# State-space stage of a hybrid layer: pieces of the first projection in every second step, nine in a row, and the next preparation in their place in the others

## The chip, the cores and the metric

The kernel runs on one core of a Trainium2 chip, as one launch. The metric is the device time of that launch in microseconds (us), the median over runs. The engines of the core work side by side, each through its own queue in order: TensorE (PE, with PEld for the loading of weights), VectorE (DVE), ScalarE (ACT), GpSimd (POOL), and SyncE (SP), which issues most DMA transfers. They wait for each other by semaphores.

## What is computed

One layer of a decoder trunk on x of 1024 tokens by 1024 channels: two branches, a gated MLP with a chunked spatial gate (y_a) and a Mamba-2 state-space mixer (y_b), are projected, gated and merged. The stage at hand is the state-space mixer, and it shares its time with the first projection, y_a @ w_proj_a. The core of the reference:

```python
def ssd_scan(x, dt, a, bmat, cmat):
    ...
    a_cs = jnp.cumsum(adt, axis=-1)
    decay = segsum_exp(adt)
    cb = jnp.einsum('bclgn,bcsgn->bcgls', cc, bc)
    y_diag = jnp.einsum('bcgls,bcgrls,bcsgrp->bclgrp', cb, decay, xd)
    decay_to_end = jnp.exp(a_cs[..., -1:] - a_cs)
    chunk_states = jnp.einsum('bcsgn,bcgrs,bcsgrp->bcgrpn', bc, decay_to_end, xd).astype(jnp.float32)
    chunk_decay = jnp.exp(a_cs[..., -1])
    def step(state, inp):
        cs, cd = inp
        return state * cd[..., None, None] + cs, state
    ...
    y_off = jnp.einsum('bclgn,bcgrpn,bcgrl->bclgrp', cc, prev_states, jnp.exp(a_cs))
    return (y_diag + y_off).reshape(b, s, h, p).astype(x.dtype)
...
    y_b = y_b + xh * d_skip[:, None]
    yz = (y_b.reshape(b, s, SSM_D_INNER) * jax.nn.silu(ssm_z)).reshape(b, s, SSM_GROUPS, SSM_D_INNER // SSM_GROUPS)
    y_b = rms_norm(yz, ssm_norm_w.reshape(SSM_GROUPS, -1)).reshape(b, s, SSM_D_INNER)
    merged = jax.nn.sigmoid(g_a) * (y_a @ w_proj_a) + jax.nn.sigmoid(g_b) * (y_b @ w_proj_b)
```

There are 8 groups of 4 heads of width 64, a state of 128, and 8 chunks of 128 tokens.

## The kernel before

**Steps.** The state-space stage goes in 32 steps, n = 0 to 31. A step is one group and two chunks (256 tokens, s = 0 to 3). Groups go in pairs: an even n is the first group of a pair, the odd n behind it the second, and s advances every second step. So n = 8r + 2s + j is group 2r + j at s; n = 10 is group 2, s = 1, and its tiles carry the ending 2_1 (yi2_1). At s = 3 (n = 6, 7, 14, 15 and so on) only one chunk state is added, since nothing follows it; at s = 0 only the second chunk has a state to read.

**Parts of a step.** `front` (L1173): PE multiplies the masked decay with the inputs (yi, 8 products, from dcy and xd) and makes the chunk states (sp, from xe and bn). The DVE adds sp to the running state (add_state, L1214 and L1216), and joins yi with the skip term into y1 (L1196); POOL multiplies the state by its chunk decay (mul_state, L1208). Where a group's squares are ready, `front` also makes the short product pq that sums them over the channels. `back` (L1220): PE makes yn from the states before each chunk, the DVE multiplies it by the decays (ym, L1242), POOL adds y1 (y, L1244) and gates the sum (yz, L1245). `prep` (L1150) readies a later step: PE makes pc (the product of C and B, and B turned) and px (x turned), the DVE multiplies the decay by pc (dcy, L1163) and px by two factors (xd, xe, L1166), and ACT copies the turned B (bn, L1170). `ahead_of` (L1543) writes, between the parts, the decay exponentials of step n+2 on ACT (L1147, eight per step; `decays(n + 3)` makes all below n+3), the state product of the next step on POOL, one of the waiting side jobs (squares on ACT, L1269; their sum on POOL, L1273; roots, L1300), and the mask of step n+3 (ACT, L1135; POOL, L1139). `fetch` (L1115) loads inputs of later steps.

**Order.** On DVE, ACT and POOL these operations are linked (`link`, L1091): each engine keeps them in the order in which they are written. PE's products stand in program order too. A scheduler places the rest. The products write to PSUM, which has 8 buffers of 512 numbers per partition; `bank` (L510) hands one out per product, six in one ring and two in another, and a product must wait until the last reader of its buffer's former tile is done.

**Pieces.** `proj_a` (L1481) is the first projection cut into pieces: each is two products of 128x128 by 128x512 into the tiles pma (192 pieces in all, 24 for each of 8 blocks). `draw` (L1534) puts some of them into the stream of PE. At the end of a block the DVE forms tha (L1506); early in a block it also makes the split weights of the next (wal, L1400, in `wa_lows`; the ACT part, L1395, in `wa_block`). The loop of before (L1557 to L1572) draws 4 pieces in an even step and 5 in an odd one, between front and back, and prepares step n+2 after back. After the loop the rest of the pieces is drawn, and the second projection (p1) begins with eight PSUM buffers taken in a written order (L1816).

Of the kernel before, what the change touches and what calls it, by code (L numbers as in the profile page):

```python
# [8 lines left out]
F32 = mybir.dt.float32  # L9
# [7 lines left out]
P = 128  # L17
# [18 lines left out]
def hybrid_kernel(  # L36
# [1444 lines left out]
    def proj_a():  # L1481

        for dd in range(KT):
            if dd + 2 < KT:
                wa_load(dd + 2)
            ths, pms = [], []
            for h in range(2):
                th = turn(tha_r, f"tha{dd}_{h}", F32)
                load(th, th_d[dd * P : (dd + 1) * P, h * 512 : (h + 1) * 512])
                ths.append(th)  # L1490
                pms.append(bank(f"pma{dd}_{h}"))
            for k in range(KT):
                wh, wl = was[dd][k // 4]
                yh, yl = yas[k]
                ks = slice(k % 4 * P, (k % 4 + 1) * P)
                for n, (lw, r) in enumerate(((wh, yh), (wh, yl), (wl, yh))):
                    for h in range(2):
                        mm(pms[h], lw[:, ks], r[h], k + n == 0, k == KT - 1 and n == 2)
                    yield
                if k == 1 and dd + 1 < KT:  # L1500
                    wa_block(dd + 1)
                elif k == 3 and dd + 1 < KT:
                    wa_lows(dd + 1)
            keep = pin if dd == KT - 1 else lambda i: i
            for h in range(2):
                keep(V.scalar_tensor_tensor(ths[h], ths[h], 1.0, pms[h], op0=ALU.add, op1=ALU.mult))  # L1506
            for h in range(2):
                keep(nc.scalar.dma_start(mt_d[dd][:, h * 512 : (h + 1) * 512], ths[h]))
# [25 lines left out]
    def draw(n):  # L1534
        for _ in range(n):
            left[0] -= next(fill, 1) is None
# [21 lines left out]
    for n in range(2):  # L1558
        step(n, "front")
        ahead_of(n)  # L1560
        draw(10)
    for n in range(len(order)):
        if n > 1:
            step(n, "front")
            ahead_of(n)
            draw(6 if n == 2 else 4 + n % 2)
        step(n, "back")
        if n == 1:
            draw(4)
        if n + 2 < len(order):  # L1570
            step(n + 2, "prep")
        fetch(n + 6)  # L1572
    while tasks or work or posts:
        draw(2)
# [238 lines left out]
    for u, (nm, k) in enumerate(units):  # L1813
        if k == 0:
            if nm == "p1":
                first = {t: psb.tile([P, 512], F32, name=f"{t}p", tag=f"b{t}") for t in ('x0', 'x1', 'x2', 'x3', 'y3', 'y1', 'y2', 'y0')}  # L1816
                psx, psy = ([first[f"{v}{j}"] for j in range(4)] for v in "xy")
            elif nm in ("p5", "p2"):
                psy = banks(f"y{nm}", "y")
            ps = psy if nm in ("p2", "p5", "p3") else psx  # L1820
        multiply(u, ps)
        ahead(u)
        if nm == "p1" and k == 2:
            for tags, _ in (y1_r, ym_r):
                room.extend(tags)
        if nm == "p1" and k in (1, 4):
            for late in groups[NG - 2 :]:
                late.post4() if k == 4 else late.post3()
            if k == 1:
                for late in groups[NG - 2 :]:  # L1830
                    late.root()
        if nm == "p2" and k == 4:
            room.extend(rb_r[0])
        if k % 2 and nm in GATES:
            gate_load(GATES[nm][0] + k // 2, GATES[nm][1])
        if nm == "p4":
            for at, f, a in BESIDE:
                if at == k:
                    f(*a)
        if nm in ("p7", "p2", "p4") and k % 2 == (nm != "p4"):  # L1840
            merged(*more.pop(0))
        if k == KT - 1:
            for j in range(4):
                with tc.high_priority():
                    if nm in ("p1", "p3", "p5"):
                        t = slot_tile(f"{nm}_{j}")
                        A.copy(t, (psx if nm == "p1" else psy)[j])
                        sums[nm, j] = t
                    if nm == "p6":
                        V.tensor_add(sums["p3", j], sums["p3", j], psx[j])  # L1850
                    elif nm == "p5":
                        V.tensor_add(sums["p3", j], sums["p3", j], sums["p5", j])
                        more.append((j, 1, sums["p3", j], f"p3_{j}"))
                    elif nm == "p7":
                        V.tensor_add(sums["p5", j], sums["p5", j], psx[j])
                        more.append((4 + j, 1, sums["p5", j], f"p5_{j}"))
                    elif nm == "p2":
                        V.tensor_add(sums["p1", j], sums["p1", j], psy[j])
                        more.append((j, 0, sums["p1", j], f"p1_{j}"))
                    elif nm == "p4":  # L1860
                        merged(4 + j, 0, None, None)
# [179 lines left out]
```

## Time and profile before

| what | value |
|---|---|
| median of 3 runs | 1365.81 us (1364.84 to 1366.97) |
| profiled execution | 1369.39 us |
| its span on the core | 1367.4 us |
| its mean granted TensorE clock | 0.998 |
| state-space steps 2 to 29 (935.15 to 1107.16) | 172.01 us |
| mean step | 172.01 / 28 = 6.14 us |

The profile shows one execution. The span is what the trace covers of its own time. A timeline row gives start, length, engine, source line, operation, output and inputs with their shapes, and in square brackets how long the engine was idle before it and what ended that. The names of the tiles are given without their numbers, so yn stands for the yn of every step. An x behind a row is the number of instructions that follow each other without a gap. A source line L82 or L85 is that of a helper that issues all products, so products are told apart by their tiles. POOL is idle in most of the span and busy in the state-space stage, so its share of the whole span says little of that stage.

### The profile page before, as it was taken

Reading aid. Unit: us, or ns where it says so; the run is one execution under the profiler, and the core shown is the slowest. Engines: PE = TensorE matmul, PEld = TensorE weight load, DVE = VectorE, ACT = ScalarE, POOL = GpSimd, SP = SyncE. Lnnn points to the kernel's source line nnn. Section 1 sums busy time; section 2 is a strip of 40 time slices with the busy share of each in tenths; the row PEclk is TensorE's granted clock in tenths of the full one; section 3 lists DMA queues with packets and bytes.
Section 4 is the critical chain, followed back from the end, with each engine's and each line's share of the span. In section 5 each row is a group of like instructions: output and inputs, shape, how many; then the busy total and the mean of one; then the engine's idle time right before and its main releaser. Section 6 shows DMA issues by size and latency. Waiting matters only on the chain.

```text
span 1367.4 us, 20180 instructions
## 1 busy us (share of the span) xinstructions
PE 1352.4 (99%) x6943; PEld 1117.4 (82%) x6943; DVE 1047.6 (77%) x1720; ACT 799.6 (58%) x1449; POOL 195.4 (14%) x191
## 2 busy tenths in 40 slices
PE   8999999999999999999999999999999999999997
PEld 7688888888888888888888888888888888888886
DVE  4786886777778898688887788457888866959976
ACT  5763666666656665465576665486877834233443
POOL 1000000000000000000000000016798971000002
PEclk9999999999999999999999999999999999999999
DMA  9675444343344657877665865488889958988913
GB/s 287 180 232 142 147 124 123 100 126 113 116 131 139 204 179 227 257 228 239 203 197 180 260 196 182 155 308 273 300 299 313 306 200 311 333 266 322 379 41 123
DMA packets 249530, 288.65 MB, mean 211 GB/s; under 512 B 16812, under 2 KB 196436, under 8 KB 249428
## 3 DMA queue, kind: packets, MB, share of 16 engines
q1 hardware_dynamic: 174868, 203.80, 46.9%
q10 hardware_dynamic: 74560, 83.57, 17.9%
q8 instruction: 55, 0.90, 0.3%
q14 instruction: 47, 0.39, 0.1%
HBM read 199.82 MB, written 87.49 MB: 210 GB/s over the span
## 4 chain that ended last, share of the span: by engine, by line
PE 90%; DVE 3%; DMA 3%; issue 1%; SPq 1%; ACT 1%; POOL 0%; POOLq 0%; DVEq 0%; ACTq 0%
PE xx L565 6%; PE xcb L565 6%; PE xz L565 6%; PE xuz L565 6%; PE xg L565 5%; PE pma L82 5%; PE ox L1885 3%; PE yuz L565 3%; PE yx L565 3%; PE ycb L565 3%; PE vx L970 3%; PE yp L1694 3%; PE yz L565 3%; PE yg L565 3%; PE yi L82 2%; PE sp L82 2%
## 5 line engine op out<-in xcount | busy, mean ns | idle before, releaser
L1139 POOL TENSOR_SCALAR_AFFINE_SELECT dcy<-dcy 128x1024 f32<-128x1024 f32 x32 | 37.7, 1179 | 788.0 <-DMA yl<-ya_d 744.6
L1147 ACT ACTIVATE dcy<-dcy,nacs 128x128 f32<-128x128 f32 x256 | 78.2, 389 | 4.9 <-POOL dcy L1139 4.2
L1163 DVE TENSOR_TENSOR dcy<-dcy,pc 128x1024 f32<-128x1024 f32 x32 | 39.0, 1220 | 9.0 <-PE pc L85 8.0
L1245 POOL TENSOR_TENSOR yz<-y,sl 128x512 f32<-128x512 f32 x32 | 44.3, 1386 | 2.5
L82 PE MATMUL pma<-yh,wah 128*128 128x512 f32 x128 | 43.1, 418 | 0.0
L82 PE MATMUL pma<-yh,wal 128*128 128x512 f32 x128 | 42.5, 413 | 0.0
L1040 ACT ACTIVATE ac<-ac 128x1024 f32<-128x1024 f32 x32 | 34.0, 1061 | 13.5 <-DVE ac L1038 13.3
L1170 ACT COPY bn<-pc 128x256 f32<-128x256 f32 x32 | 11.9, 372 | 49.8 <-DVE dcy L1163 49.8
L1632 DVE SCALAR_TENSOR_TENSOR yn<-yn,par,rb 128x512 f32<-128x512 f32 x32 | 25.2, 786 | 20.1 <-DMA yn<-yb_d 18.8
L82 PE MATMUL pma<-yl,wah 128*128 128x512 f32 x128 | 40.2, 395 | 0.0
L1135 ACT ACTIVATE ea<-dcy 64x512 f32<-64x512 f32 x64 | 39.8, 622 | 0.4
L1244 POOL TENSOR_TENSOR y<-y,ym 128x512 f32<-128x512 f32 (+1 forms) x32 | 37.0, 1156 | 3.5 <-DVE ym L1242 3.1
L1038 DVE SCALAR_TENSOR_TENSOR ac<-c2x,cwt,ac 128x1023 f32<-128x1023 f32 (+2 forms) x24 | 30.7, 1280 | 7.3 <-ACT ac L1036 7.2
L1038 DVE SCALAR_TENSOR_TENSOR ac<-c2cb,cwt,ac 128x1023 f32<-128x1023 f32 (+2 forms) x24 | 30.7, 1280 | 6.8 <-ACT ac L1036 6.6
L1242 DVE TENSOR_TENSOR ym<-yn,ea 128x512 f32<-128x512 f32 (+1 forms) x32 | 19.9, 623 | 19.9 <-PE yn L82 19.7
L82 PE MATMUL yi<-dcy,xd 128*64 128x128 f32 x512 | 35.0, 279 | 0.0
L82 PEld LDWEIGHTS yn<-sl,st 128*128 128x128 f32 x224 | 30.4, 195 | 5.3 <-POOL st L1208 2.8
L1900 POOL TENSOR_TENSOR r<-r,fnw 128x512 f32<-128x512 f32 x4 | 5.3, 1342 | 204.4 <-ACT junk L1898 204.4
L82 PE MATMUL yn<-sl,st 128*128 128x128 f32 x224 | 30.9, 278 | 2.4 <-POOL st L1208 2.4
L840 ACT CAST wbb<-wbr 128x512 fp32r<-128x512 f32 x32 | 19.8, 618 | 22.5 <-DMA wb_d<-wbb 18.9
L82 PE MATMUL sp<-xe,bn 128*128 128x256 f32 x112 | 32.7, 409 | 0.0
L1002 ACT ACTIVATE vm<-vm,vr 128x128 f32<-128x128 f32 x64 | 25.7, 483 | 11.3 <-DMA vm<-v_d 10.9
(2975 smaller groups left out, 4380.2 us busy)
## 6 DMA issues: line engine op xcount, KB each, us to landing
sl<-s_d SPq DMA_DIRECT2D x32, 768.0 KB, 6.7
s_d<-ac ACTq DMA_DIRECT2D x32, 512.0 KB, 3.6
wb_d<-wbb ACTq DMA_DIRECT2D x32, 512.0 KB, 3.6
dcy<-acs_d SPq DMA_DIRECT2D x32, 512.0 KB, 5.6
av<-in_w_in_dram SPq DMA_DIRECT2D x36, 256.0 KB, 3.2
aw<-in_ada_w_dram SPq DMA_DIRECT2D x16, 512.0 KB, 6.5
wbr<-in_w_proj_b_dram SPq DMA_DIRECT2D x32, 256.0 KB, 4.6
yb_d<-yz ACTq DMA_DIRECT2D x32, 256.0 KB, 6.0
```

The costliest lines, as they stand in the source:

```text
L82: pin(PE.matmul(acc, l, r, start=first, stop=last))
L565: pin(PE.matmul(ps, lw[:, k * P : (k + 1) * P], r[k], start=first and n + k == 0, stop=n == 2 and k == 3, skip_group_check=not first))
L970: pin(PE.matmul(ps[pn][j], l[:, j * P : (j + 1) * P], r, start=nm in ("p1", "p5", "p2") and n + units[i][1] == 0, stop=n == 2 and k == 3, ...
L1038: V.scalar_tensor_tensor(ac[:, s:], cc[:, : S - s], conv_wt[:, 3 - s, i : i + 1], ac[:, s:], op0=ALU.mult, op1=ALU.add)
L1135: link("A", lambda: A.activation(ea[hh * HD : (hh + 1) * HD], dcy.rearrange("p (j e) i l -> p e j (i l)", e=2)[hh * HD : (hh + 1) * HD, hh ...
L1139: link("G", lambda: G.affine_select(out=d8, in_=d8, compare_op=ALU.is_ge, fill=-1e30, base=0, pattern=[[0, 2 * HPG], [1, P]], channel_mult ...
L1147: link("A", lambda: A.activation(dcy[:, h, i, :], dcy[:, h, i, :], AF.Exp, bias=sub[:, i, h : h + 1]))
L1163: link("V", lambda: V.tensor_tensor(d3, d3, pc[:, 0:256].unsqueeze(1).to_broadcast([P, HPG, 256]), op=ALU.mult))
L1244: link("G", lambda: G.tensor_add(y1[:, :, t0:], y1[:, :, t0:], m[:, :, t0:]))
L1245: link("G", lambda: G.tensor_mul(yz, y1, sl[:, 4:6]))
L1694: pin(PE.matmul(ps[j], a[:, v, js], r, start=first and n + k == 0, stop=n == 2 and k == KT - 1, skip_group_check=not first))
L1885: pin(PE.matmul(ps, a[:, tsl], b[:, cs], start=first and n + j == 0, stop=n == 2 and j == 3, skip_group_check=not first))
```

## The change

The main loop treats even and odd steps apart from n = 2 on. An even step draws no piece; there the preparation of step n+2 stands between `ahead_of` and `back`. An odd step draws nine pieces (eleven at n = 3) between front and back, and prepares step n+2 after back as before. Through the loop as many pieces are drawn as before, and no operation is added or removed on any engine. For the first block alone the split of the next block's low weights is written after the sixth instead of the fourth eighth of the block. And the eight buffers of the second projection are taken in another order.

```diff
-                elif k == 3 and dd + 1 < KT:
+                elif k == (3 if dd else 5) and dd + 1 < KT:
                     wa_lows(dd + 1)
...
+    def prepare(n):
+        if n < len(order):
+            step(n, "prep")
+
     for n in range(len(order)):
+        even = n > 1 and n % 2 == 0
         if n > 1:
             step(n, "front")
             ahead_of(n)
-            draw(6 if n == 2 else 4 + n % 2)
+        if even:
+            prepare(n + 2)
+        elif n > 1:
+            draw(11 if n == 3 else 9)
         step(n, "back")
         if n == 1:
             draw(4)
-        if n + 2 < len(order):
-            step(n + 2, "prep")
+        if not even:
+            prepare(n + 2)
         fetch(n + 6)
...
-                first = {t: psb.tile([P, 512], F32, name=f"{t}p", tag=f"b{t}") for t in ('x0', 'x1', 'x2', 'x3', 'y3', 'y1', 'y2', 'y0')}
+                first = {t: psb.tile([P, 512], F32, name=f"{t}p", tag=f"b{t}") for t in ('x0', 'x1', 'y3', 'x2', 'y0', 'y2', 'y1', 'x3')}
```

Three places show what this does to the engines. The first is PE in step 10. Before, the chunk states sp2_1 are followed by four pieces, then yn of the step, then the preparation of step 12 (pc2_2):

```order
L82 MATMUL sp2_1_9173<-xe2_1_9079,bn2_1_9081 128x256 x2
L82 MATMUL pma2_0_8812<-yh60_8166,wal2_1_8566 128x512
L82 MATMUL pma2_1_8815<-yh61_8167,wal2_1_8566 128x512
L82 MATMUL pma2_0_8812<-yh70_8172,wah2_1_8565 128x512
L82 MATMUL pma2_1_8815<-yh71_8173,wah2_1_8565 128x512
L82 MATMUL pma2_0_8812<-yl70_8174,wah2_1_8565 128x512
L82 MATMUL pma2_1_8815<-yl71_8175,wah2_1_8565 128x512
L82 MATMUL pma2_0_8812<-yh70_8172,wal2_1_8566 128x512
L82 MATMUL pma2_1_8815<-yh71_8173,wal2_1_8566 128x512
L82 MATMUL yn2_1_9205<-sl2_1_8851,st22_8278 128x128 x2
L82 MATMUL yn2_1_9205<-sl2_1_8851,st_8275 128x128 x2
L82 MATMUL pc2_2_9217<-sl2_2_9007 128x128
```

In the changed kernel, from the same product on:

```order
L82 MATMUL sp2_1_9173<-xe2_1_9061,bn2_1_9063 128x256 x2
L82 MATMUL pc2_2_9198<-sl2_2_9007 128x128
L85 MATMUL pc2_2_9198<-ident_135,sl2_2_9007 128x128
L85 MATMUL px2_2_9197<-ident_135,sl2_2_9007 128x128 x2
L82 MATMUL pc2_2_9198<-sl2_2_9007 128x128
L85 MATMUL pc2_2_9198<-ident_135,sl2_2_9007 128x128
L85 MATMUL px2_2_9197<-ident_135,sl2_2_9007 128x128 x2
L82 MATMUL yn2_1_9214<-sl2_1_8851,st22_8278 128x128 x2
L82 MATMUL yn2_1_9214<-sl2_1_8851,st_8275 128x128 x2
L82 MATMUL yi3_1_9230<-dcy3_1_8912,xd3_1_9151 64x128 x8
L82 MATMUL pq0_1_9239<-yz0_2_8744,ones_140 32x128 x4
L82 MATMUL sp3_1_9246<-xe3_1_9153,bn3_1_9155 128x256 x2
```

The four pieces are gone from between sp and yn, the preparation of step 12 stands there, and yi of step 11 follows yn directly; pq0_1 is the sum of squares that the front of step 11 makes.

The second place is the DVE in the same step, from the skip term y1 of step 10 on. Before:

```order
L1196 SCALAR_TENSOR_TENSOR y12_1_9178<-sl2_1_8851,dskt_151,yi2_1_9164 128x256 x2
L1506 SCALAR_TENSOR_TENSOR tha2_0_8810<-tha2_0_8810,pma2_0_8812 128x512
L1506 SCALAR_TENSOR_TENSOR tha2_1_8813<-tha2_1_8813,pma2_1_8815 128x512
L1216 TENSOR_TENSOR st21_8277<-st21_8277,sp2_1_9173 128x256
L1242 TENSOR_TENSOR ym2_1_9210<-yn2_1_9205,ea2_1_8853 128x512
L1163 TENSOR_TENSOR dcy2_2_9005<-dcy2_2_9005,pc2_2_9217 128x1024
L1166 TENSOR_TENSOR xd2_2_9227<-px2_2_9216,dthq_154 128x512
L1166 TENSOR_TENSOR xe2_2_9229<-px2_2_9216,dde_155 128x512
```

In the changed kernel:

```order
L1196 SCALAR_TENSOR_TENSOR y12_1_9178<-sl2_1_8851,dskt_151,yi2_1_9164 128x256 x2
L1216 TENSOR_TENSOR st21_8277<-st21_8277,sp2_1_9173 128x256
L1163 TENSOR_TENSOR dcy2_2_9005<-dcy2_2_9005,pc2_2_9198 128x1024
L1166 TENSOR_TENSOR xd2_2_9208<-px2_2_9197,dthq_154 128x512
L1166 TENSOR_TENSOR xe2_2_9210<-px2_2_9197,dde_155 128x512
L1242 TENSOR_TENSOR ym2_1_9219<-yn2_1_9214,ea2_1_8853 128x512
L1285 TENSOR_SCALAR cwt_148<-pq0_1_9239 128x128
L1216 TENSOR_TENSOR st_8275<-st_8275,sp3_1_9246 128x256
L1196 SCALAR_TENSOR_TENSOR y13_1_9251<-sl3_1_8914,dskt_151,yi3_1_9230 128x256 x2
```

The three operations on the preparation of step 12 (dcy2_2, xd2_2, xe2_2), which stood behind ym of step 10, now stand ahead of it, and so ahead of the state and y1 of step 11 as before; the two tha of the block have moved behind those.

The third place is POOL around the sum of squares of group 3 (yz3_0, L1273), in steps 15 and 16. Before:

```order
L1273 TENSOR_TENSOR yz2_0_9061<-yz2_0_9061 128x512
L1139 AFFINE_SELECT dcy5_0_9419<-dcy5_0_9419 128x1024
L1244 TENSOR_TENSOR y12_3_9515<-y12_3_9515,ym2_3_9547 128x512
L1245 TENSOR_TENSOR yz2_2_9394<-y12_3_9515,sl2_3_9161 128x2x256
L1300 TENSOR_TENSOR ssq_158<-ssq_158,nhalf_144 128x8
L1139 AFFINE_SELECT dcy4_1_9498<-dcy4_1_9498 128x1024
L1244 TENSOR_TENSOR y13_3_9594<-y13_3_9594,ym3_3_9626 128x512
L1245 TENSOR_TENSOR yz3_2_9474<-y13_3_9594,sl3_3_9235 128x2x256
L1208 TENSOR_TENSOR st21_8277<-st_8275,cd_157 128x256
L1273 TENSOR_TENSOR yz3_0_9135<-yz3_0_9135 128x512
```

In the changed kernel:

```order
L1300 TENSOR_TENSOR ssq_158<-ssq_158,nhalf_144 128x8
L1139 AFFINE_SELECT dcy5_0_9403<-dcy5_0_9403 128x1024
L1244 TENSOR_TENSOR y12_3_9515<-y12_3_9515,ym2_3_9556 128x512
L1245 TENSOR_TENSOR yz2_2_9397<-y12_3_9515,sl2_3_9161 128x2x256
L1273 TENSOR_TENSOR yz2_0_9068<-yz2_0_9068 128x512
L1139 AFFINE_SELECT dcy4_1_9498<-dcy4_1_9498 128x1024
L1244 TENSOR_TENSOR y13_3_9579<-y13_3_9579,ym3_3_9620 128x512
L1245 TENSOR_TENSOR yz3_2_9474<-y13_3_9579,sl3_3_9227 128x2x256
L1208 TENSOR_TENSOR st21_8277<-st_8275,cd_157 128x256
L1273 TENSOR_TENSOR yz3_0_9135<-yz3_0_9135 128x512
```

The sum of group 2's squares (yz2_0) and a root (ssq, L1300) have changed places: the sum now stands one step later, only five operations ahead of the sum of group 3.

## The prediction

> **What bounds the kernel now.** I read the page first: its span and its busy row for TensorE.
>
> ```profile
> span 1367.4 us, 20180 instructions
> PE 1352.4 (99%) x6943; PEld 1117.4 (82%) x6943; DVE 1047.6 (77%) x1720; ACT 799.6 (58%) x1449; POOL 195.4 (14%) x191
> ```
>
> TensorE sets the end, so the change can win only TensorE work or TensorE waits. The windows view, over the stretch that the change rearranges (start of step 2 to start of step 30; the columns are length, PE, PEld, DVE, ACT, POOL, clock, DMA share, GB/s), and the waits view for PE around it (905 to 1130) say what is there to win:
>
> ```profile
> 935.15:1107.16 172.01, 172.01 (x1381) 146.74 (x1380) 142.75 (x254) 128.81 (x342) 148.14 (x145) 1.00 0.87 294
> ...
> PE yn L82 <- POOL st L1208: 2.4, 1, 2.4
> PE pq L82 <- POOL lq L1265: 0.3, 1, 0.3
> ```
>
> PE is busy for all 172.01 us, 172.01 / 28 = 6.14 us a step, at the full granted clock. The two waits lie outside (at 928 and in the tail). VectorE and GpSimd, at 83% and 86% of the stretch, are close behind. So the state-space loop holds no wait that the change could remove, and two engines have less than 1.1 us of slack a step.
>
> **How a step is paced.** The timeline of step 10, which starts at T = 984.21 with its yi, up to the first products of step 11:
>
> ```profile
> 984.15 1.22 DVE L1163 TENSOR_TENSOR dcy<-dcy,pc 128x1024 f32<-128x1024 f32 x1 [0.51 <-PE pc L85]
> 984.21 1.09 PE L82 MATMUL yi<-dcy,xd 128*64 128x128 f32 x16
> 984.59 1.09 POOL L1139 TENSOR_SCALAR_AFFINE_SELECT dcy<-dcy 128x1024 f32<-128x1024 f32 x1 [2.36 <-ACT ea L1135]
> 985.23 1.13 PE L82 MATMUL sp<-xe,bn 128*128 128x256 f32 x4
> 985.29 0.68 DVE L1166 TENSOR_TENSOR xd<-px,dthq 128x512 f32<-128x512 f32 x1
> 985.41 0.37 ACT L1170 COPY bn<-pc 128x256 f32<-128x256 f32 x1 [0.89 <-DVE dcy L1163]
> 985.80 1.15 ACT L1269 ACTIVATE yz<-yz 128x512 f32<-128x512 f32 x2
> 985.89 0.68 DVE L1166 TENSOR_TENSOR xe<-px,dde 128x512 f32<-128x512 f32 x1
> 986.01 0.81 PE L82 MATMUL pma<-yh,wal 128*128 128x512 f32 x2
> 986.46 1.30 POOL L1245 TENSOR_TENSOR yz<-y,sl 128x512 f32<-128x512 f32 x1
> 986.65 0.63 PE L82 MATMUL pma<-yh,wah 128*128 128x512 f32 x2
> 986.86 2.14 ACT L1147 ACTIVATE dcy<-dcy,nacs 128x128 f32<-128x128 f32 x7
> 987.12 0.62 PE L82 MATMUL pma<-yl,wah 128*128 128x512 f32 x2
> 987.71 1.18 POOL L1208 TENSOR_TENSOR st<-st,cd 128x256 f32<-128x256 f32 x2
> 988.04 1.05 PE L82 MATMUL yn<-sl,st 128*128 128x128 f32 x8
> 988.86 1.28 POOL L1273 TENSOR_TENSOR yz<-yz 128x512 f32<-128x512 f32 x1
> 988.91 0.39 ACT L1147 ACTIVATE dcy<-dcy,nacs 128x128 f32<-128x128 f32 x1
> 988.93 0.39 PE L82 MATMUL pc<-sl 128*128 128x128 f32 x2
> 990.13 1.09 PE L82 MATMUL yi<-dcy,xd 128*64 128x128 f32 x16
> 991.15 0.43 PE L82 MATMUL pq<-yz,ones 128*32 128x128 f32 x8
> ```
>
> From starts to starts: yi and sp take 986.01 - 984.21 = 1.8 us, a pair of pieces' rows 0.47 (986.65 to 987.12), yn 0.89 (988.04 to 988.93), a preparation (pc, px) 1.20 (988.93 to 990.13), yi alone 1.02 (990.13 to 991.15). The pieces are the cover: while PE multiplies them, ScalarE makes the decays of step 12 (done at 988.91 + 0.39 = 989.30 = T+5.09), which the DVE needs for the preparation of step 12 (PE does it at T+4.72, DVE right behind). GpSimd works through its queue without a gap up to 990.14 = T+5.93.
>
> **The change, part by part.** The same products, copies and pieces run, so no engine's work changes. What changes is where TensorE has cover. An even step now goes yi, sp, preparation, yn with no piece: 1.8 + 1.2 + 0.9 = 3.9 us, say 4.0, until yi of the next step, and 5.0 until what follows that yi. The odd step gets nine pieces, 18 rows or some 4.2 us, and is 8.2 us long. The preparation of n+2 is asked of PE at T+1.9 instead of T+4.7, but its DVE and ACT part can't come earlier: the decay of n+2 is finished at T+5.09 where squares (L1269) stand before it, and without them as in step 4, where T is 948.37:
>
> ```profile
> 948.37 1.09 PE L82 MATMUL yi<-dcy,xd 128*64 128x128 f32 x16
> 949.96 1.28 ACT L1147 ACTIVATE dcy<-dcy,nacs 128x128 f32<-128x128 f32 x4
> ...
> 943.45 2.45 ACT L1147 ACTIVATE dcy<-dcy,nacs 128x128 f32<-128x128 f32 x8
> ```
>
> that is at 949.96 + 2.45 = 952.41 = T+4.04. Behind it come dcy (1.14 from start to start), xd (0.60), xe (0.68), and bn (0.37) on ACT. So the buffer of px is free only at T+6.5 (7.5 with squares) and that of pc at about T+5.7 (6.6). Meanwhile PE hands out PSUM buffers at twice the pace, and ym(n), which waits only for yn, is now queued behind that trio on the DVE. In the built order each product takes a certain buffer; these are the places where its last reader is late, and the stalls they give:
>
> Step 10: pq0_1 takes the buffer of px2_2, the preparation just made. Wanted at T+5.0; free at 5.09 + 1.14 + 0.60 + 0.68 = T+7.5. 2.4 us; and px2_2 itself takes that of px3_1, whose xe ends at 985.89 + 0.68 = T+2.36, wanted at T+2.2: 0.2.
>
> Step 28: sp7_2, in the front of step 29, takes the buffer of px6_3. Wanted at T+5.4, since a pq (0.43) stands in step 28's front; free at T+6.5: 1.1 us.
>
> Step 26: sp7_1, in the front of step 27 behind a pq, takes the buffer of pc6_2: wanted at T+5.4, bn at T+6.6. 1.2 us.
>
> Steps 16 and 24: the pq in the odd step's front is now wanted at T+5.0, and the sum (L1273) it reads is the last of GpSimd's queue; in step 10 that ended at T+5.93, at 16 and 24 it starts later because the y product before it waited for the late ym and another sum stands ahead: 0.9 at least, 1.28 + 0.9 = 2.2 at most, 1.4 taken for each: 2.8 us. Steps 18 and 26 have the same with one sum: 0.3 each, 0.6.
>
> Step 20: the pc of step 22 takes the buffer of step 21's px: its xe at T+2.4 to T+2.8 against T+2.2: 0.4.
>
> Steps 2, 6 and 30 need rows of their own, of the timeline in step 2 (T = 935.15) and step 30 (T = 1107.16):
>
> ```profile
> 935.15 1.09 PE L82 MATMUL yi<-dcy,xd 128*64 128x128 f32 x16
> 938.12 0.37 ACT L1170 COPY bn<-pc 128x256 f32<-128x256 f32 x1 [5.21 <-DVE dcy L1163]
> 939.20 0.41 DVE L1216 TENSOR_TENSOR st<-st,sp 128x256 f32<-128x256 f32 x1
> 939.53 0.86 DVE L1196 SCALAR_TENSOR_TENSOR y<-sl,dskt,yi 128x256 f32<-128x256 f32 x2
> ...
> 1107.16 1.09 PE L82 MATMUL yi<-dcy,xd 128*64 128x128 f32 x16
> 1108.54 0.81 PE L82 MATMUL pma<-yh,wal 128*128 128x512 f32 x2
> 1109.45 0.41 DVE L1216 TENSOR_TENSOR st<-st,sp 128x256 f32<-128x256 f32 x1
> 1109.78 0.86 DVE L1196 SCALAR_TENSOR_TENSOR y<-sl,dskt,yi 128x256 f32<-128x256 f32 x2
> ```
>
> Step 2, where the DVE comes late from earlier work: yn is wanted at T+3.0 and takes the buffer of pc (bn ends at 938.49 = T+3.34), its second half waits for the state (939.61 = T+4.46), and the next yi for y1 (940.39 = T+5.24). 0.3 + 0.7 + 0.3 = 1.3 us. Step 6, a short front like step 30's: PE is through yi and sp at T+1.4, through the preparation at T+2.6, and yn takes the buffer of its own yi, which y1 frees at 1110.64 = T+3.48: 0.9. Step 30 has no preparation left: yn follows at T+1.4, its second half at T+1.85 waits for the state at 1109.86 = T+2.70: 0.85.
>
> The sum is 2.4 + 0.2 + 1.1 + 1.2 + 2.8 + 0.6 + 0.4 + 1.3 + 0.9 + 0.85 = 11.75 us. A stalled pair of steps starts the next pair late on all engines alike, so a stall isn't paid back by the odd step: PE has no gap there to give up. The other side: 14 fewer runs of pieces. The first pair of a run shows 986.65 - 986.01 = 0.64 instead of 0.47 us, 0.17 more; but it begins while the rows of sp still run (985.23 + 1.13 = 986.36), so most of that is overlap. Between 0 and 14 x 0.17 = 2.4 us I take 0.6, near the low end. The later wal subtractions of the second block, the tail's first buffers and the fetches add no instruction and no transfer, and leave PE's products in place: nothing, and 1 us at most for a late first product of the tail. That makes 11.75 - 0.6 = +11.1 us. Against the profiled execution's span it is 1367.4 + 11.1 = 1378.5 (1380.5 with what lies around it, 1369.39); against the median of the runs, 1365.81, it is 1376.9.
>
> **A stall may cost more than itself.** After the one long wait of before, the rows ran at half rate:
>
> ```profile
> 928.37 1.17 PE L82 MATMUL yn<-sl,st 128*128 128x128 f32 x4 [2.38 <-POOL st L1208]
> 929.32 0.63 PE L82 MATMUL pc<-sl 128*128 128x128 f32 x2
> 929.75 0.42 PE L85 MATMUL pc<-ident,sl 128*128 128x128 f32 x1
> 932.02 0.70 PE L82 MATMUL pma<-yh,wal 128*128 128x512 f32 x2
> ```
>
> pc's pair took 929.75 - 929.32 = 0.43 us to the next product, where a whole preparation of 10 such rows takes 1.20. From 928.4 to 932.0 work went at half speed, some 1.6 us lost for 2.38 us idle. The Trainium skill, "TensorE: Matmul & The Clock Gate", section "HAM oscillation — how this bites in real kernels", gives an idle gap above about 3.4 us as what brings the slow clock. By that rule none of the stalls summed here would cost clock. By the row above, the one at step 10 (2.4 us) might, and the sum would be 1378.5; the rule is not borne out by that row.
>
> **The rivals.** First, stalls that drop the clock: three of them (steps 10, 16, 24) at 1.6 us: 1376.9 + 4.8 = 1381.7. For it speaks the row after 2.38 us; against it that only one stall is as long as that.
>
> Second, all is hidden, 1365.8: were the decays of n+2 made a step sooner, px and pc would be free in time. ACT has 172.01 - 128.81 = 43 us of idle time for that, but its order is written, the decay behind bn of the step before, and the sums on GpSimd would stay late; it decides if the trio on the DVE is done by T+5.0.
>
> Third, faster: the start of a run is a real loss on PE, halving the 28 runs brings the whole 2.4 us, the 0.3 us wait of pq in the tail goes too, and the buffers are free in time after all: 1365.8 - 2.7 = 1363.1. It decides where the stalls together stay under 2.7 us. For it speaks the 0.17 us in the row, against it the overlap.
>
> Fourth, a part of it: only the waits for buffers of px and pc and for the states stay and GpSimd's are hidden, since its queue may run ahead: 11.1 - 3.4 = 7.7: 1373.5. This is part of my forecast's own range.
>
> **How the numbers follow.** The forecast, slower without loss of clock, has 0.62 (the fourth case in it); with loss of clock 0.17; hidden 0.09; faster 0.12. A difference of 0.2%, 2.7 us, is about what a measurement of this kernel tells from none. The third case ends at that bound, so 0.08 of it counts as faster and 0.04 as the same: faster 0.08, same 0.13, slower 0.79. The likeliest one's own range is 1371 (the stalls half as long) to 1381 (each GpSimd wait at its bound of 2.2). It is widened to the clock case above, and below until the hidden and the faster case are left out, which with what lies above make two in ten: 1368.5 to 1384.
>
> **What would show it.** In the profile after, PE's waits in this stretch should be some 9 to 14 us instead of none: pq on the DVE's xe (L1166) with about 2.4 us, pq on GpSimd's L1273 twice over 1 us, yn on the DVE's L1216 and L1196, sp on bn and xe in the last steps; each pair of steps 12.3 us plus its stalls, and the stretch from step 2 to step 30 about 182 us. A granted clock under 1.00 there would show the clock case. If waits stay under 3 us, the forecast is wrong at its root, that the late decay holds the buffers; if they are there but the time isn't longer, the start of a run of pieces was mis-sized.

## The result, and the profile after

| | before | after |
|---|---|---|
| median of the runs (5 each, in turn on one chip) | 1365.81 us (1364.84 to 1366.97) | 1379.44 us (1378.70 to 1380.84) |
| profiled execution | 1369.39 us | 1379.44 us |
| its span | 1367.4 us | 1377.6 us |

The changed kernel takes 1.0098 of the time (95% interval 1.0086 to 1.0109), 13.6 us more. The forecast was 1376.9 us, within 1368.5 to 1384.0. The busy row of the changed kernel's page:

```profile
PE 1354.2 (98%) x6943; PEld 1118.1 (81%) x6943; DVE 1048.9 (76%) x1720; ACT 800.1 (58%) x1449; POOL 191.6 (14%) x191
```

TensorE does as many products as before, 1.8 us more of busy time, and its share falls from 99% to 98%: the rest is waiting. The waits view for PE over 931 to 1125, where before had none but the 0.3 us in the tail (columns: total, times, longest):

```profile
PE pq L82 <- DVE xe L1166: 2.3, 1, 2.3
PE pq L82 <- POOL yz L1273: 2.3, 2, 1.3
PE yn L82 <- DVE y L1196: 1.5, 1, 1.5
PE sp L82 <- DVE xe L1166: 1.4, 1, 1.4
PE sp L82 <- ACT bn L1170: 1.1, 1, 1.1
PE yn L82 <- DVE st L1216: 1.0, 2, 0.6
PE pc L82 <- PE sp L82: 0.7, 1, 0.7
PE yn L82 <- ACT bn L1170: 0.2, 1, 0.2
```

They sum to 10.5 us, in ten single stalls, each where a buffer, a state or a sum came late. The windows view of the changed kernel shows where they fall: first the stretch from step 2 to step 30, then the pairs of steps that begin with 4, 10 and 28.

```profile
931.39:1116.71 185.32, 175.14 (x1381) 148.35 (x1380) 144.54 (x254) 128.81 (x342) 147.80 (x145) 0.99 0.82 277
946.22:958.48 12.26, 12.26 (x96) 10.70 (x95) 10.94 (x18) 9.51 (x25) 9.39 (x10) 1.00 0.88 285
983.71:1000.39 16.68, 14.36 (x103) 11.84 (x102) 12.19 (x21) 9.59 (x25) 11.62 (x13) 0.90 0.64 218
1102.70:1116.71 14.01, 12.64 (x103) 10.85 (x102) 9.43 (x18) 7.72 (x22) 11.10 (x12) 1.00 0.62 217
```

The same three pairs before:

```profile
948.37:960.66 12.29, 12.29 (x95) 10.64 (x94) 10.42 (x19) 9.09 (x25) 8.47 (x10) 1.00 0.98 325
984.21:996.85 12.64, 12.64 (x103) 10.79 (x102) 11.35 (x21) 9.81 (x26) 11.71 (x12) 1.00 0.71 233
1094.52:1107.16 12.64, 12.64 (x103) 10.80 (x102) 9.52 (x18) 7.83 (x22) 11.45 (x13) 1.00 0.68 241
```

The stretch grew from 172.01 to 185.32 us, by 13.3: PE is idle for 185.32 - 175.14 = 10.2 us of it, and its busy time grew by 3.1, of which 1.7 in pair 10 (14.36 against 12.64). A pair without a stall (4) takes as long as before, pair 28 grew by its one wait of 1.4 us, and pair 10 by 4.0 us, the only one with a granted clock under 1.00. The timeline of the changed kernel in step 10 (T = 983.71) shows why:

```profile
983.71 1.09 PE L82 MATMUL yi<-dcy,xd 128*64 128x128 f32 x16
...
985.30 1.15 ACT L1269 ACTIVATE yz<-yz 128x512 f32<-128x512 f32 x2
...
986.36 2.43 ACT L1147 ACTIVATE dcy<-dcy,nacs 128x128 f32<-128x128 f32 x8
...
988.00 1.09 PE L82 MATMUL yi<-dcy,xd 128*64 128x128 f32 x16
...
988.82 1.22 DVE L1163 TENSOR_TENSOR dcy<-dcy,pc 128x1024 f32<-128x1024 f32 x1 [1.28 <-ACT dcy L1147]
...
990.56 0.68 DVE L1166 TENSOR_TENSOR xe<-px,dde 128x512 f32<-128x512 f32 x1
...
991.39 0.66 PE L82 MATMUL pq<-yz,ones 128*32 128x128 f32 x8 [2.29 <-DVE xe L1166]
...
991.98 2.08 PE L82 MATMUL sp<-xe,bn 128*128 128x256 f32 x4
...
994.64 0.63 PE L82 MATMUL pma<-yh,wah 128*128 128x512 f32 x2
```

Without pieces PE is through step 10 and the yi of step 11 at T+5.3, while ACT finishes the decay of step 12 at 988.79 = T+5.08. The DVE's dcy, xd and xe stand behind it, and pq takes the buffer that xe reads last: 2.29 us idle. Then sp takes 2.08 us where before's row has 1.13: the stall has cost clock too. From start to start, yi to pq takes 991.39 - 988.00 = 3.39 us where yi alone takes 1.02, so this stall costs 2.37 us; the rows of PE hide some hundredths of each, because a product's row covers the start of the gap behind it.

### The profile page after: what moved, and what is told of

It reads as the page before. It is cut to its first block, busy times and chain, and to the rows that moved or that the text cites. A ratio compares the mean times of both kernels' runs of the same rounds, so it can differ in the third digit from the quotient of the medians.

```text
span 1377.6 us, 20179 instructions
## 1 busy us (share of the span) xinstructions
PE 1354.2 (98%) x6943; PEld 1118.1 (81%) x6943; DVE 1048.9 (76%) x1720; ACT 800.1 (58%) x1449; POOL 191.6 (14%) x191
## 5 line engine op out<-in xcount | busy, mean ns | idle before, releaser
L1245 POOL TENSOR_TENSOR yz<-y,sl 128x512 f32<-128x512 f32 x32 | 41.4, 1293 | 2.5
L82 PE MATMUL pma<-yh,wah 128*128 128x512 f32 x128 | 40.3, 396 | 0.0
L1002 ACT ACTIVATE vm<-vm,vr 128x128 f32<-128x128 f32 x64 | 25.7, 484 | 11.1 <-DMA vm<-v_d 10.6
L1038 DVE SCALAR_TENSOR_TENSOR ac<-c1cb,cwt,ac 128x1023 f32<-128x1023 f32 (+2 forms) x24 | 30.7, 1278 | 1.3 <-ACT ac L1036 1.3
```

The costliest lines, as they stand in the source:

```text
L82: pin(PE.matmul(acc, l, r, start=first, stop=last))
L1002: A.activation(vn[:, cs], vn[:, cs], AF.Identity, scale=vr[:, 1, ch : ch + 1], bias=vr[:, 2, ch : ch + 1])
L1038: V.scalar_tensor_tensor(ac[:, s:], cc[:, : S - s], conv_wt[:, 3 - s, i : i + 1], ac[:, s:], op0=ALU.mult, op1=ALU.add)
L1245: link("G", lambda: G.tensor_mul(yz, y1, sl[:, 4:6]))
```

## The experiments

Groups of runs share a chip and its runs of the kernel before. Stretch is the time from the start of step 2 to that of step 30 in the profiled execution, against 172.0 us in before.

| kernel | median, us | before beside it | ratio (95%) | stretch |
|---|---|---|---|---|
| before again, one run | 1368.07 | 1368.14 | | 172.0 |
| loop alone | 1382.48 | 1368.14 | 1.0105 (1.0083 to 1.0126) | 184.7 |
| preparation alone | 1382.56 | 1368.14 | 1.0107 (1.0087 to 1.0127) | 176.8 |
| pieces alone | 1384.36 | 1368.14 | 1.0115 (1.0099 to 1.0131) | 186.2 |
| after again | 1380.34 | 1365.80 | 1.0106 (1.0091 to 1.0122) | 184.0 |
| preparation alone, other tail order | 1372.95 | 1365.80 | 1.0059 (1.0042 to 1.0075) | 177.2 |
| two pieces kept | 1378.14 | 1365.80 | 1.0091 (1.0076 to 1.0106) | 181.6 |
| decay sooner | 1378.32 | 1365.80 | 1.0094 (1.0079 to 1.0109) | 182.9 |
| other ring turn | 1380.47 | 1365.28 | 1.0113 (1.0100 to 1.0126) | 183.8 |
| before, subtractions later | 1368.57 | 1365.28 | 1.0022 (1.0013 to 1.0031) | 172.0 |

**Before again.** The unchanged kernel, for what its profile does from one execution to another.

> The kernel before, once more, for a second profile of it. In the first one the execution took 1369.39 us, 3.6 more than the median of its runs, and PE waited 2.38 us at 928 and then ran at half rate. If that wait belongs to that one execution: no such wait here, a time of 1365 to 1367, and the change's cost is about 13.5 us, all of it between step 2 and step 30. If it belongs to the kernel: the wait is here again, and the change takes 3.7 us of wait away there and costs more elsewhere.

Its stretch is the same 172.0 us, and its long wait of PE ahead of step 2 came again.

**Loop alone.** The main loop of the change; the two small edits undone.

```diff
-                elif k == (3 if dd else 5) and dd + 1 < KT:
+                elif k == 3 and dd + 1 < KT:
...
-                first = {... for t in ('x0', 'x1', 'y3', 'x2', 'y0', 'y2', 'y1', 'x3')}
+                first = {... for t in ('x0', 'x1', 'x2', 'x3', 'y3', 'y1', 'y2', 'y0')}
```

> The change without its two small parts: the low weights of the second block after the fourth eighth, and the tail's buffers in the order of before. Theory (cover lost in the even steps): these parts are worth nothing within 1 us, 1379 to 1380. Rival: the new order of the tail's buffers makes up for, or costs, some us at the join to the second projection; then the time differs from 1379.4 by over 2 us.

The loop holds the whole loss: its stretch is 184.7 us and its ratio lies within the interval of the full change. Its median is 3 us above the 1379.4 of the change, but the kernel before ran 2.3 us longer in that group too. Its timeline at the place of the 2.3 us stall:

```profile
993.84 0.43 PE L82 MATMUL pq<-yz,ones 128*32 128x128 f32 x8 [2.29 <-DVE xe L1166]
994.20 1.13 PE L82 MATMUL sp<-xe,bn 128*128 128x256 f32 x4
...
995.62 0.63 PE L82 MATMUL pma<-yh,wah 128*128 128x512 f32 x2
```

The same idle time to 0.01 us, and no slow rows. From the start of pq to the first wah pair it takes 995.62 - 993.84 = 1.78 us, in the changed kernel 994.64 - 991.39 = 3.25: the clock cost 1.47 us there.

**Preparation alone.** The early preparation stays, but the even steps have their four and the odd ones their five pieces again, behind it.

```diff
-        elif n > 1:
-            draw(11 if n == 3 else 9)
+        if n > 1:
+            draw(6 if n == 2 else 4 + n % 2)
```

> Even steps prepare step n+2 ahead of back, as in the change, but the pieces stay four and five a step. Theory: with 1.9 us of pieces behind it the early preparation is mostly covered; left are PE's waits at step 10 (pq on xe, about 1.1 us), step 28 (sp on xe, 0.9) and some tenths for pq on the sums of GpSimd, 3 to 5 us in all: 1369 to 1371, and no loss of clock. Rival (the early preparation by itself holds the buffers): over 1375. Rival (the preparation's place doesn't matter at all): 1365 to 1367.

The stretch lost 4.8 us, within the 3 to 5 expected, but the kernel as much as with the full change, some 10 us more than expected. The timeline and the windows view (granted clock third from the right) show the rest in the tail:

```profile
1142.90 0.80 PE L1702 MATMUL x2p<-p1bh,p1a 128*128 128x512 f32 x1 [5.91 <-DVE tha L1506]
...
1141.39:1148.22 6.83, 5.32 (x13) 4.16 (x14) 6.53 (x11) 2.07 (x4) 3.42 (x2) 0.50 0.63 186
```

The eight buffers of the second projection were taken in the changed kernel's order. With other products in the ring, x2p got a buffer whose last reader, the end of a block, was far behind: 5.9 us, and half the clock for 6.83 us around its end. That order has to be fitted to each loop.

**Preparation alone, other tail order.** The same, with the buffers in the order in which this loop frees them.

```diff
-                first = {... for t in ('x0', 'x1', 'y3', 'x2', 'y0', 'y2', 'y1', 'x3')}
+                first = {... for t in ('x1', 'x0', 'y2', 'y1', 'y0', 'x2', 'y3', 'x3')}
```

> As prep_alone (pieces four and five, early preparation in even steps), but the tail's buffers in the order in which they come free here. In prep_alone the second projection's third product waited about 7 us for such a buffer. Theory: 4 to 6 us over the kernel before, all of it in the steps, 1.003 to 1.0045. Rival (the tail's order wasn't it): 12 us and more over it.

The stall is gone, and 7.2 us remain, a little over the 4 to 6 expected, 5.2 of them in the stretch, whose longest waits of PE are:

```profile
PE pq L82 <- POOL yz L1273: 1.3, 3, 0.9
PE pq L82 <- DVE xe L1166: 1.1, 1, 1.1
PE sp L82 <- DVE xe L1166: 0.8, 1, 0.8
```

These are kinds of waits of the changed kernel, each about half as long: an early preparation costs something even where the pieces cover PE.

**Pieces alone.** No piece in the even steps and nine in the odd ones, but every preparation behind `back` as before.

```diff
-        if even:
-            prepare(n + 2)
-        elif n > 1:
+        if n > 1 and not even:
             draw(11 if n == 3 else 9)
...
-        if not even:
-            prepare(n + 2)
+        prepare(n + 2)
```

> No piece in even steps, nine in odd ones, but the preparation stays behind back in every step. Theory: yn follows sp directly in every even step, and its second half waits for the state add, as at step 30: 0.3 to 0.9 us in each of 14 steps, 2.4 at step 2, 11 us in all: 1375 to 1379; the waits of pq on xe are gone and no wait but step 2's passes 1 us. Rival (the early preparation is what costs): 1365 to 1368.

The stretch lost 14.2 us, more than with the full change and 3 more than expected, and the waits view of PE shows another wait:

```profile
PE yn L82 <- DVE st L1216: 8.2, 8, 2.3
...
PE yn L82 <- DVE st L1214: 2.0, 3, 0.7
```

Here yn follows sp at once, and its second half waits until the DVE has added sp to the state. So the preparation in the place of the pieces is not what costs most; it covers some of what the missing pieces laid open. The two parts, 5.2 and 14.2 us, don't add up to the 13.3 of both.

**Two pieces kept.** Two pieces behind the early preparation in an even step, seven in an odd one, with a tail order of its own.

```diff
         if even:
             prepare(n + 2)
+            draw(2)
         elif n > 1:
-            draw(11 if n == 3 else 9)
+            draw(9 if n == 3 else 7)
```

> The change with two pieces left in each even step, between preparation and back, and seven in each odd one; the tail's buffers in their order here. Theory (cover): 0.9 us more of it before yn takes 0.9 from each stall: pq on xe at step 10 1.3 instead of 2.3 (and no half clock), sp on xe and bn in the last steps about 1 and 0.3, the waits of steps 2 and 6 nearly gone; 6 us in all over the kernel before, 1.004 to 1.006. Rival (what costs is that the steps alternate, not the length of the cover): above 1.0075.

9.6 us in the stretch, not the 6 expected, and a ratio of 1.0091, past the 1.0075 that the expectation gave to its rival, that the steps alternate. Of the long waits one shrank by the 0.94 us that two pieces cover (2.3 to 1.4), another, sp on xe in the front of step 29, not at all:

```profile
PE sp L82 <- DVE xe L1166: 1.4, 1, 1.4
PE pq L82 <- DVE xe L1166: 1.4, 1, 1.4
```

With 0, 2 and 4 pieces in an even step the stretch loses 13.3, 9.6 and 5.2 us: about 2 us for each piece taken from the 14 even steps of the stretch. The sp of step 29 shows why a piece of 0.47 us doesn't take 0.47 us off every stall: with the two pieces GpSimd's state product (L1208) and the DVE's state behind it end later in step 28, and so does xe. No run takes pieces from the even steps without adding them to the odd ones, so the rival isn't excluded by itself; what speaks for cover is that the long waits have a late reader in the rows.

**Decay sooner.** If the late decay holds the buffers, it should help to make it sooner: the odd steps from 3 on write the mask of step n+3 earlier and that step's decays right behind it, one step ahead of their time, so that an even step finds the decay made of the step that it prepares. The tail order was fitted again.

```diff
-            decays(n + 3)
+            if n < 3 or n % 2 == 0:
+                decays(n + 3)
+            else:
+                masks(n + 4)
+                decays(n + 4)
```

> The change, with the decays of step n+3 made already in the odd step n, behind the mask, so that ACT has no decay to make in an even step before the early preparation; the tail's buffers in their order here. Theory (the late decay is what holds the buffers of px and pc): pq on xe at step 10 falls from 2.3 to about 1 (the squares still stand ahead), sp on bn at step 26 goes, GpSimd's sums are earlier; steps 2, 6, 30 and sp at step 28 stay: 6 to 7 us over the kernel before, 1.004 to 1.006. Rival (the order on the DVE or PSUM's turn holds them, whatever ACT does): within 2 us of the change itself, above 1.008.

The stretch still lost 10.9 us where 6 to 7 were expected, and the ratio of 1.0094 lies where the expectation put its rival, that the DVE's order or the ring holds the buffers whatever ACT does. The windows view of pairs 10 and 14, and the timeline in step 10 (T = 984.71):

```profile
984.71:998.56 13.85, 12.90 (x104) 10.87 (x103) 11.59 (x21) 11.42 (x32) 12.01 (x13) 1.00 0.65 217
1011.42:1025.42 14.00, 12.21 (x92) 9.96 (x91) 9.46 (x16) 12.10 (x34) 12.33 (x11) 1.00 0.76 235
```

```profile
987.32 0.86 DVE L1196 SCALAR_TENSOR_TENSOR y<-sl,dskt,yi 128x256 f32<-128x256 f32 x2
...
988.13 0.42 DVE L1216 TENSOR_TENSOR st<-st,sp 128x256 f32<-128x256 f32 x1
...
990.20 0.68 DVE L1166 TENSOR_TENSOR xe<-px,dde 128x512 f32<-128x512 f32 x1
...
991.03 0.43 PE L82 MATMUL pq<-yz,ones 128*32 128x128 f32 x8 [0.92 <-POOL dcy L1139]
```

Pair 10 fell from 16.68 to 13.85 us and at full clock: 1.4 of its 2.3 us wait were the late decay. The other 0.9 stay, and the buffer still explains them: pq doesn't read the mask that the view names, and it starts 0.15 us behind the end of xe (990.88), as in the changed kernel (991.24 to 991.39). What stands ahead of dcy now, without a gap, is the DVE's own work: y1 and the second state addition, behind which dcy starts at 988.47. In step 28 it is the same, and sp still waits 1.2 us there. The 1.1 us on bn in step 26 and the waits on GpSimd's sums are gone. But pair 14, which takes 11.42 in the changed kernel, now has 14.00, and the timeline ahead of it shows why:

```profile
1008.73 1.27 ACT L1135 ACTIVATE ea<-dcy 64x512 f32<-64x512 f32 x2 [2.49 <-DMA dcy<-acs_d]
...
1013.01 0.69 DVE L1400 TENSOR_TENSOR wal<-wa,wah 128x512 fp32r<-128x512 f32 x1 [3.58 <-ACT wah L1395]
...
1014.36 0.49 PE L82 MATMUL pc<-sl 128*128 128x128 f32 x2 [1.22 <-DVE ym L1242]
```

The early mask is asked for before its input has landed, so ACT stands for 2.49 us; 2.45 us of decays follow, and only then the cast wah, for which the DVE waits 3.58 us with ym behind it. The work that was put forward stands in the way of other work.

**Other ring turn.** The same loop and the same products, but each takes another buffer: the smaller ring gets the fourth instead of the third of every four.

```diff
-            if len(pairs_done) % 4 == 2:
+            if len(pairs_done) % 4 == 3:
```

> The change with another turn of the PSUM buffers: the call that takes one of the two px buffers is the fourth of each four instead of the third, so that every late reader stands in another product's way; the tail's buffers in their order here. Theory (it is the late readers, and which product meets them is only the turn): pq at step 10 waits for GpSimd's sum alone (0.3 to 1 us) and the half clock behind it is gone, pair 10 takes 13 to 13.5 us instead of 16.8; but pc at steps 22 and 30 now meets y1 of the step (1 to 1.5 us each), yn at step 2 meets xe; 10 to 12 us between step 2 and step 30 over the kernel before, 1.007 to 1.010. Rival (the particular turn makes the loss): less than 6 us there.

The stretch lost 11.8 us, as expected, at other places; the kernel as a whole, 1.0113, lies above the 1.007 to 1.010 expected. Pair 10 in the windows view, and two rows of PE's waits:

```profile
983.38:996.17 12.79, 12.71 (x104) 10.86 (x103) 10.41 (x19) 9.61 (x25) 10.52 (x12) 1.00 0.70 238
```

```profile
PE pc L82 <- issue: 2.8, 2, 1.4
...
PE yn L82 <- DVE xe L1166: 1.9, 2, 1.1
```

Pair 10 lost its stall and runs 0.15 us over before's 12.64; yn inherits the late xe, and two pc wait 1.4 us each for something that the profile doesn't name (issue). Which product waits is a matter of the ring; the loss of the stretch as a whole hardly is.

**After again, and before with two subtractions later.** Both are for the head of the stage. In the profile of before PE waits 2.4 us ahead of step 2 for the state, in that of the changed kernel it doesn't. The timeline of before, at step 0:

```profile
916.50 3.51 POOL L1139 TENSOR_SCALAR_AFFINE_SELECT dcy<-dcy 128x1024 f32<-128x1024 f32 x1 [18.63 <-ACT ea L1135]
916.57 2.50 DVE L1378 TENSOR_TENSOR yl<-yl,yh 128x512 fp32r<-128x512 f32 x4
```

and of the changed kernel, with the same two operations:

```profile
916.83 1.09 POOL L1139 TENSOR_SCALAR_AFFINE_SELECT dcy<-dcy 128x1024 f32<-128x1024 f32 x1 [18.63 <-ACT ea L1135]
916.91 3.36 DVE L1378 TENSOR_TENSOR yl<-yl,yh 128x512 fp32r<-128x512 f32 x4
```

GpSimd's mask and the DVE's four subtractions start within 0.1 us of each other, and one of the two is long. To see whether this belongs to the change, the changed kernel was run again, and in before the last two subtractions were moved behind step 0's skip term (tail order fitted):

```diff
-            pin(V.tensor_sub(yl[i], f32(yl[i]), f32(yh[i])))
+            if k < 7:
+                pin(V.tensor_sub(yl[i], f32(yl[i]), f32(yh[i])))
...
+        if n == 0:
+            yh7, yl7 = yas[7]
+            with tc.high_priority():
+                for i in range(2):
+                    link("V", lambda: V.tensor_sub(yl7[i], f32(yl7[i]), f32(yh7[i])))
```

> The changed kernel once more, beside the kernel before on one chip. In its first profile GpSimd's mask at 916.8 took 1.09 us and the DVE's four subtractions beside it 3.36; in the five other profiles so far the mask took 3.5 and the subtractions 2.50, and PE then waited 2.4 us at yn. Theory: which of the two engines goes first is a matter of the execution, not of the change, and the change costs 13 to 14 us where both kernels fall alike. Then this profile may show either, and the time is 1.008 to 1.011 of the kernel before. Rival: the change always lets GpSimd go first; then it does so again, and step 10 has the half clock again.

> The kernel before, with the last two of the DVE's four subtractions at 916 (yl of the last eighth) moved behind the first step's state and skip term, so that GpSimd's mask meets two of them and not four; the tail's buffers in their order here. Theory (the two engines keep each other out while these run, and the order between them is chance): the mask takes at most 2.3 us instead of 3.5 in the bad case, PE's 2.4 us wait at yn shrinks to about 1, and the first yi to step 2 takes 18 to 20 us in every execution; 1 to 2 us less than the kernel before in the median, 0.998 to 1.0005. Rival: the pieces of that eighth come late instead and PE waits for them: 1.001 or more.

After again had the 2.4 us wait (yn on POOL's L1208): one kernel shows both. Its pair 10 was slow a second time, 16.84 us at a granted clock of 0.90, while its pair 2 took 13.30 us instead of 14.83: where the head comes late, step 2 waits less.

Moving the subtractions took the 2.4 us wait away but made before slower, 1.0022, as the rival of the expectation had it: the pieces of that eighth of the block now wait for them, as its timeline shows:

```profile
925.86 1.10 PE L82 MATMUL pma<-yl,wah 128*128 128x512 f32 x2 [1.51 <-DVE yl L1565]
```

No kernel of this study beats before.

## Why the prediction was right, and where its terms were off

The direction, the place and the kind of the loss were as forecast, and the median came 2.5 us above the predicted 1376.9. By its own steps:

- **No wait to win, cover lost.** Right. The stretch grew by 13.3 us (182 us in all were foreseen, 185.3 came), and two experiments tie that to the pieces: kept in the even steps they bring it back by some 2 us each, and with the pieces gone alone it is 14.2.
- **Step 10, 2.4 us for pq on xe.** 2.29, or 2.37 from starts, at the product named; the 0.2 for px is there too, from 985.92 to 986.22 where 0.11 is usual. (From T+5.0 to T+7.5 would be 2.5; the forecast wrote 2.4. PE came at T+5.3 and the buffer at T+7.7.) The forecast kept the loss of clock as a rival and out of the sum; here it came, 1.47 us, and again in after again, but not in loop alone after the same 2.29. As a rival it had three stalls at 1.6; one of them fell so.
- **Steps 16 and 24, 1.4 us each for GpSimd's sums.** 0.97 and 1.28 us, 2.3 for 2.8. The 0.6 for steps 18 and 26 didn't come: the waits list has two such waits only. The forecast's upper end of its own range, 1381, rests on these waits at 2.2 each, and doesn't come out of that: with the two of steps 16 and 24 at 2.2 the sum gives 1378.5.
- **Steps 26 and 28, sp on bn and on xe.** 1.13 and 1.37 us against 1.2 and 1.1. At step 28 the late decay was not alone: ACT finished it at 1106.55, and the DVE's state, which waited for GpSimd, stood ahead of dcy until 1107.04. So sp still waits 1.2 us there with the decay sooner.
- **Steps 2, 6 and 20.** Step 6 waited 1.50 for its skip term instead of 0.9; step 20's pc 0.7 for 0.4 (the view names sp there; the xe that was forecast ends just ahead, at 1053.45, and pc starts at 1053.54); pair 2 grew from 13.22 to 14.83 us, 1.6 for 1.3, but in after again, behind a late head, by 0.1 only.
- **Fewer starts of runs of pieces, 0.6 won.** Nothing to see: pair 4 takes 12.26 against 12.29 us. The term was taken from a row that overlaps the product before it; its lower bound was the right one. What the pieces no longer pay, the preparation does: behind sp they start after 0.78 us, pc only after 0.97 (984.73 to 985.70 in step 10), which the forecast's 1.8 us for yi and sp left out.
- **The decays' lateness as the cause.** Only in part, and this is where the forecast's mechanism was too narrow. Decay sooner took 1.4 us and the loss of clock off step 10 and ended the wait on bn, but elsewhere the skip term and the state hold PE by themselves, and on the DVE they stand ahead of the preparation. The rival "all is hidden" hung on the DVE's trio (dcy, xd, xe) being done by T+5.0 with the decay sooner; in step 10 it was done at T+6.2, behind y1 and the state. What that rival named as staying late, the sums on GpSimd, left no wait. The loss of 10.9 us shows how little that edit alone is worth.
- **The rivals.** "Faster" needed stalls of under 2.7 us together; they are 10.5. The fourth, with GpSimd's part hidden, falls with the 2.3 us on its sums.
- **The sum.** 11.75 - 0.6 = 11.1 us were forecast, 0.85 of it in step 30, which lies behind the stretch; from there to the tail the time grew by 0.8. So 10.3 stand against 13.3. Of the 3.0 missing, 0.6 are the starts that won nothing. The rest comes out of the lengths of the pairs, growth less forecast: pair 10 is 1.4 over (the clock), pair 6 0.8, pair 20 0.5, pairs 2 and 28 0.3 each, while the pairs from 14 to 18 and from 22 to 26 are 0.8 under. So the sum is as near as it is partly because terms that were too small met others that were too large.
- **The base.** The profile of before, at 1369.39 us, lay above all five of its runs (1364.84 to 1366.97). It had the 2.4 us wait and slow rows in its head, but so had before again, and no profile of before shows a head without them; that they are the difference is not shown. The head (step 0's first product to step 2's) took 22.6 us there, and 18.5 in the changed kernel's. So the two spans differ by 10.2 us only: 13.3 + 0.8 - 4.1 is 10.0. Before again and after again, whose heads are alike at 22.5, differ by 1379.8 - 1366.2 = 13.6 us of span, as the medians do: 12.0 in the stretch, 0.7 behind it, and 1.0 ahead of step 0, where the change moves nothing. That the two agree to the tenth is in part chance.
- **The tail's buffers at nothing.** True of the change, whose order fits its loop. It is not nothing in itself: 5.9 us in preparation alone.

That the loss comes from one cause alone isn't shown, and missing cover in the even steps was never tried apart from longer runs in the odd ones. What is shown: the loop holds all of it, each of its two parts alone is slower than before, the loss falls with each piece that is put back, and the waits move with the ring while the loss of the stretch hardly does (13.3 and 11.8 us).

## What to carry to other kernels

Independent products between two dependent parts of a step are cover; gathering them into one long run leaves the other steps open, and a run twice as long paid nothing back here. To price such a move, follow each product to the buffer it takes, find that buffer's last reader in the timeline, and compare the two times; it gave the places and most of the sizes here. Look also at what stands ahead of that reader on its own engine: making one late input sooner only brings out the next. After any edit of such a loop, fit the order in which the next stage takes its buffers, or a stall of several microseconds hides what the edit itself does; and read a single execution's base with its own accidents taken out.

## What the runs showed of the hardware

**The clock falls after idle times under 2.4 us, and not each time.** Idle for 2.29 us, PE ran at half rate in the changed kernel and in after again, and at full rate in loop alone. The windows view gives the granted clock (third from the right): first the changed kernel around its stall, then loop alone around the same one:

```profile
987.73:991.14 3.41, 1.37 (x20) 1.00 (x18) 2.32 (x3) 2.58 (x7) 2.25 (x2) 1.00 0.85 342
991.14:994.56 3.42, 3.17 (x14) 2.36 (x15) 1.41 (x5) 3.40 (x10) 2.53 (x2) 0.50 0.02 7
```

```profile
988.71:992.12 3.41, 2.83 (x31) 2.47 (x31) 2.13 (x5) 3.40 (x11) 2.41 (x3) 1.00 0.92 322
992.12:995.54 3.42, 1.70 (x14) 1.39 (x15) 2.58 (x6) 2.60 (x9) 2.26 (x2) 1.00 0.29 119
```

The half rate lasts 3.41 us, and it starts 0.25 us before pq does, while PE is still idle. In before it lasts 3.41 us as well (928.46 to 931.87). In the trace's record of the clock every stretch at half rate in these runs begins a whole multiple of 3.41 us after the clock first rose (288 times 3.41 in the changed kernel, 270 times in before). The Trainium skill, "TensorE: Matmul & The Clock Gate", section "What's actually happening", describes a window of 3.4 us that runs freely, so that it depends on where in it work begins. The rows agree. Cut into such windows, the stall of the changed kernel lies almost whole in one, with PE busy for 1.37 us, and that of loop alone is divided between two, with 2.83 and 1.70. The rule of that section of the Trainium skill, that an idle time of about 3.4 us is needed, doesn't hold for these rows. How little work brings the fall isn't settled: in this stage the clock fell behind windows with 1.0 to 1.4 us of work and held behind one with 1.56 (two pieces kept), but fell behind one with 1.80 (before with two subtractions later); the ends of PE's rows are modelled, so these sums are not exact.

**The DVE and GpSimd shut each other out.** The four subtractions take 2.50 us alone and 3.36 beside a mask that starts 0.08 us earlier; the mask takes 1.09 us, or 3.51 behind the subtractions. In before they end at 919.07 and the mask at 920.01, 0.94 us later, nearly its own length. With the subtractions split, in the timeline of before with two subtractions later, a single one, of 0.68 us otherwise, lasts until 0.55 us after the mask's end at 917.76:

```profile
916.67 1.09 POOL L1139 TENSOR_SCALAR_AFFINE_SELECT dcy<-dcy 128x1024 f32<-128x1024 f32 x1 [18.62 <-ACT ea L1135]
916.76 1.55 DVE L1379 TENSOR_TENSOR yl<-yl,yh 128x512 fp32r<-128x512 f32 x1
```

The Trainium skill, "SBUF — State Buffer", section "SBUF: two separate sides", describes a pair of ports that one of the two holds for a whole instruction while the other is blocked. The rows agree, and show one thing more: the mask didn't get in between four subtractions in a row. Who comes first changes from execution to execution, though the mask's row starts first both times. It decides 2.4 us in the head of this stage, and 4.0 where the clock falls behind the wait: the head takes 18.5 us in the changed kernel, 20.9 in loop alone, which had the wait but no half clock, and 22.5 in after again, which had both.
